# Merging the up-projection tiles and loading their gate tiles as side steps

## The chip, the cores and the metric

The kernel runs on one core of a Trainium2 chip. The metric is the device time of one launch in microseconds (us). The engines named here are TensorE (PE for its matmuls, PEld for its weight loads), VectorE (DVE), ScalarE (ACT), GpSimd (POOL) and SyncE (SP), which issues most of the DMAs.

## The reference

The reference is one decoder block in float32: 512 tokens, model width 2048. The part that matters here stands at its end. Two branches, retention and sparse attention, each give an array of 512 x 1024. Each is widened to 2048 columns, multiplied by its own sigmoid gate, and the two are added:

```
merged = sigmoid(m_a) * (y_ret @ w_up_ret) + sigmoid(m_b) * (y_nsa @ w_up_nsa)
x = x + gate[:, None] * (merged @ w_out)
return rmsnorm(x, g_final)
```

`gate` is a third of a projection of the conditioning vector `c` through `w_ada`.

## The kernel before, in words

**Stages.** The kernel first forms the modulated input, then streams the input projection through TensorE group by group, with the two attention branches worked off beside it; then comes the up stage, which the change touches, and then the output projection. Every large product is done as three products of rounded parts: a weight is split into a high part `whi` (ACT rounds it, L261) and a low part `wlo` (DVE subtracts, L262), and a product is high x high, high x low and low x high (L414).

**The up stage (L1005 to L1020).** It has eight groups, in the order j = 0 to 3 and, for each j, first w = 1 (sparse attention, weights `w_un`) and then w = 0 (retention, weights `w_ur`). A group makes four result tiles `u` of 128 channels x 512 tokens in four PSUM banks. It uses four weight tiles of 128 x 1024 (512 KB), called W1 to W4 below, and each holds two of the eight contraction steps. So a group is 4 tiles x 8 steps x 3 = 96 matmuls. `run_group` (L431) does them in three blocks: W1 alone, W2 alone, then W3 and W4 together (tail=2). A block (L423) runs four steps, one per result tile; after each step it calls `tick`. In the last block each step closes its tile, and the evacuation `ev` of that tile is written out at once.

**Evacuation (L990 to L1003).** For w = 1 it is one DVE product, `mtmp = u * sg` (L993). For w = 0 it is the product `sg = u * sg` (L996), the sum into `mtmp` (L997), ACT's rounding to the high part `mhi` (L1000) and DVE's subtraction to the low part (L1001); for j of 2 and 3 POOL then stores the low part to DRAM (L1003).

**The gates' tiles.** `sg` is a tile of 256 KB with the sigmoid of one gate, which the input projection stored to DRAM in `ma_d`. Each group loads its four `sg` tiles on SP's queue (L1017) before its first block is written out. They share four buffers, so the load of one waits until the evacuation of the tile before it in that buffer has read it.

**The gate column.** Between the weights of the up stage stand 32 more tiles of 512 KB, four in each group, called g1 to g4 below. Each is one DVE step into `gacc` (L987).

**What sets the order.** Each engine works off its queue in the order of the program. `load` (L218, issue at L236) keeps up to five raw 512 KB tiles in flight or in use, in the order W1 g1 W2 g2 W3 g3 W4 g4; a load is written out as soon as a buffer has been taken before it, and on the chip it waits until that use is over. `split` (L251) keeps three pairs of `whi`, `wlo`. Written out, block 1 splits W2 and W3, block 2 splits W4, and block 3 splits W1 of the next group; g1 follows block 1, g2 and g3 follow block 2, g4 follows block 3. SP's loads are written out g3 at block 1, W4 and g4 at g1, the next W1 with block 2, the next g1 and W2 behind it, the next g2 at block 3, the next W3 at g4.

**Side steps.** `side` is a queue of functions. `tick(w)` (L377) adds rate x w to a credit, which is never above 2.0, and runs one side step for each whole credit; `flush` (L383) runs what is left. `tick` is called with w = 1 in blocks 1 and 2 and with w = 2 in block 3. In the kernel before, the queue is empty throughout the up stage; the output projection fills it with four loads of `x` and four short products of the gate column, at a rate of 0.5.

Of the kernel before, what the change touches and what calls it, by code (L numbers as in the profile page):

```python
# [16 lines left out]
OP = mybir.AluOpType  # L17
# [68 lines left out]
def block_kernel(ctx: ExitStack, tc: tile.TileContext, t_in, out):  # L86
    nc = tc.nc
# [14 lines left out]
    def gbank(name):  # L102
        return bank("pg", 4, name)
# [10 lines left out]
    def bigt(name, dt=F32):  # L114
        return big.tile([P, 8, 512], dt, tag="big", name=name)
# [256 lines left out]
    side = deque()  # L372
    credit = [0.0]
    RATE_N, RATE_R = 0.32, 0.2
    rate = [0.0]
# [7 lines left out]
    def flush():  # L383
        while side:
            side.popleft()()
# [45 lines left out]
    def run_group(grp, idx, n, between=None, tail=2):  # L431

        items = []
        done = 0
        while done < n:
            if plan[idx][0] not in "wh":
                between(idx, plan[idx])
                idx += 1
                continue
            items.append(idx)  # L440
            idx += 1
            done += 1
            if done <= n - tail or done == n:
                grp.block(items)
                items = []
        while idx < len(plan) and plan[idx][0] not in "wh":
            between(idx, plan[idx])
            idx += 1
        return idx
# [524 lines left out]
    y_lo["r"] = bigt("ylo_r", F32R)  # L974
    for h in range(RH):
        nc.gpsimd.dma_start(y_lo["r"][:, h, :], yl_d[0, h])
    m_hi = [None, None]
    m_lo = [None, None]

# [10 lines left out]
    def up_evac(w, j, sgs):  # L990
        def ev(t, b):
            if w:
                nc.vector.tensor_tensor(mtmp[:, t, :], b, sgs[t], op=OP.mult)  # L993
                return
            a, k8 = divmod(4 * j + t, 8)
            nc.vector.tensor_tensor(sgs[t], b, sgs[t], op=OP.mult)  # L996
            nc.vector.tensor_tensor(mtmp[:, t, :], sgs[t], mtmp[:, t, :], op=OP.add)  # L997
            hs = m_hi[a][:, k8, :]
            ls = wk.tile([P, 512], F32R, tag="p", bufs=3, name=f"ml{j}{t}") if a else m_lo[0][:, k8, :]
            nc.scalar.copy(hs, mtmp[:, t, :])  # L1000
            nc.vector.tensor_tensor(ls, mtmp[:, t, :], hs.bitcast(F32), op=OP.subtract)  # L1001
            if a:
                nc.gpsimd.dma_start(ml_d[k8], ls)  # L1003
        return ev

    for j in range(4):
        if j % 2 == 0:
            m_hi[j // 2] = bigt(f"mhi{j}", F32R)
            if j == 0:
                m_lo[0] = bigt("mlo0", F32R)  # L1010
        for w in (1, 0):
            bk = [gbank(f"u{j}{w}_{t}") for t in range(4)]
            yh, yl = y_hi["n" if w else "r"], y_lo["n" if w else "r"]
            sgs = []
            for t in range(4):
                sg = wk.tile([P, 512], F32, tag="ev", bufs=4, name=f"sg{j}{w}{t}")
                nc.sync.dma_start(sg, ma_d[w, 4 * j + t])  # L1017
                sgs.append(sg)
            grp = Group("F", bk, lambda kk, y=yh: y[:, kk, :], lambda kk, y=yl: y[:, kk, :], 8, up_evac(w, j, sgs))
            idx = run_group(grp, idx, 4, gate_item)  # L1020


    m_lo[1] = bigt("mlo1", F32R)
# [146 lines left out]
```

## Time and profile before

| | us |
|---|---|
| median of 3 runs (1617.72 to 1619.35) | 1617.76 |
| the profiled execution's own time | 1619.62 |
| its span, first to last instruction | 1617.9 |
| PE busy in it | 1588.0 (98%) |
| DVE busy | 712.6 (44%) |
| ACT busy | 489.2 (30%) |
| the up stage, first to last product, start to start | 1253.10 to 1429.78 |

The profile's page tells busy time per engine and the chain of work that ended last; it is 90% PE. Beside the page, the trace can be asked for the waits between engines, for the instructions of one engine in order of time with the idle time ahead of each, and for the busy time, granted TensorE clock and DMA rate of any stretch. Matmuls are pipelined, so the distance between the starts of two matmuls, not the length of one, tells how fast they follow each other. An SP row gives the time for which SP issued a transfer; the landing is later.

### The profile page before, as it was taken

The numbers are of one execution on the slowest core, as the hardware profiler recorded it, in microseconds if no ns is written. First come the engines' busy times: TensorE is split into PE (matmuls) and PEld (weight loads), VectorE is DVE, ScalarE is ACT, GpSimd is POOL, SyncE is SP. The second block draws the span as 40 slices with busy tenths as digits, with TensorE's granted clock in tenths as the row PEclk, the third lists the DMA queues.
The fourth block names the chain that finished last, engine by engine and source line by source line (L and its number), as shares of the span: only waits on it lengthen the run. The fifth ranks groups of instructions, "written<-read, shape, count | busy, mean of one in ns | idle before, by whom it ended". The sixth has DMA issues, their size and how long they took to land.

```text
span 1617.9 us, 18828 instructions
## 1 busy us (share of the span) xinstructions
PE 1588.0 (98%) x7502; PEld 1266.3 (78%) x7502; DVE 712.6 (44%) x1238; ACT 489.2 (30%) x719; POOL 33.9 (2%) x68
## 2 busy tenths in 40 slices
PE   7999999999999999999999999999999999999997
PEld 2566777888888888778888888888888888778886
DVE  5454533345534344542245343332221566654444
ACT  1223313234433534432333333332222222222223
POOL 2000000000000000000001000000001000010000
PEclk9999999999999999999999999999999999999999
DMA  9886354323323313213544554333335777884322
GB/s 373 325 312 222 112 172 152 105 91 106 103 72 98 105 59 98 92 59 111 172 143 134 178 179 147 122 124 124 112 112 167 271 230 236 260 297 182 104 79 105
DMA packets 88217, 252.54 MB, mean 156 GB/s; under 512 B 9248, under 2 KB 18528, under 8 KB 86976
## 3 DMA queue, kind: packets, MB, share of 16 engines
q1 hardware_dynamic: 80048, 235.71, 42.5%
q0 software_dynamic: 7504, 13.53, 2.7%
q10 hardware_dynamic: 576, 2.10, 0.3%
q8 instruction: 59, 0.97, 0.2%
q14 instruction: 30, 0.25, 0.0%
HBM read 224.03 MB, written 27.26 MB: 155 GB/s over the span
## 4 chain that ended last, share of the span: by engine, by line
PE 90%; DVE 4%; DMA 3%; ACT 2%; issue 1%; SPq 0%; ACTq 0%; DVEq 0%
PE g L414 58%; PE o L414 11%; PE u L414 6%; PE g L879 2%; PE o L719 2%; PE sc L682 2%; PE pa L324 2%; PE tp L705 1%; PE ssq L272 1%; PE phid L603 1%; DMA raw<-in_w_ada 1%; DVE wlo L262 1%; DMA raw<-in_w_un 1%; DMA raw<-in_w_ur 1%; PE o L716 1%
## 5 line engine op out<-in xcount | busy, mean ns | idle before, releaser
L262 DVE TENSOR_TENSOR wlo<-raw,whi 128x1024 fp32r<-128x1024 f32 x246 | 297.9, 1223 | 487.0 <-ACT whi L261 486.9
L414 PE MATMUL g<-hhi,whi 128*128 128x512 f32 x1088 | 438.2, 403 | 0.0
L414 PE MATMUL g<-hhi,wlo 128*128 128x512 f32 x1088 | 424.8, 390 | 1.6 <-DVE wlo L262 1.6
L414 PE MATMUL g<-hlo,whi 128*128 128x512 f32 x1088 | 424.1, 390 | 0.0
L261 ACT CAST whi<-raw 128x1024 fp32r<-128x1024 f32 x246 | 255.0, 1048 | 499.8 <-PE g L414 229.0
L414 PEld LDWEIGHTS g<-hhi,whi 128*128 128x128 f32 x1088 | 204.7, 188 | 56.2 <-issue 11.6
L414 PEld LDWEIGHTS g<-hhi,wlo 128*128 128x128 f32 x1088 | 204.5, 188 | 46.4 <-DVE wlo L262 2.5
L414 PEld LDWEIGHTS g<-hlo,whi 128*128 128x128 f32 x1088 | 204.8, 188 | 42.9 <-issue 1.4
L414 PE MATMUL g<-whi,hhi 128*128 128x512 f32 x320 | 133.8, 418 | 0.0
L414 PE MATMUL g<-wlo,hhi 128*128 128x512 f32 x320 | 124.9, 390 | 1.2 <-DVE wlo L262 1.2
L414 PE MATMUL g<-whi,hlo 128*128 128x512 f32 x320 | 125.0, 391 | 0.0
L414 PE MATMUL o<-whi,mhi 128*128 128x512 f32 x240 | 95.0, 396 | 0.0
L414 PE MATMUL o<-wlo,mhi 128*128 128x512 f32 x240 | 93.5, 390 | 0.0
L414 PE MATMUL o<-whi,mlo 128*128 128x512 f32 x240 | 93.4, 389 | 0.0
L414 PEld LDWEIGHTS g<-wlo,hhi 128*128 128x128 f32 x320 | 60.2, 188 | 16.7 <-issue 2.4
L414 PEld LDWEIGHTS g<-whi,hhi 128*128 128x128 f32 x320 | 60.1, 188 | 15.8 <-issue 3.2
L414 PEld LDWEIGHTS g<-whi,hlo 128*128 128x128 f32 x320 | 60.0, 188 | 13.0
L685 DVE CUSTOM_DVE_ANT_0 p<-sc,c_mask 128x128 f32<-128x128 f32 (+3 forms) x64 | 31.2, 488 | 85.3 <-PE sc L682 85.2
L706 ACT COPY pT<-tp 128x128 f32<-128x128 f32 (+3 forms) x64 | 27.3, 426 | 114.6 <-PE tp L705 114.4
L687 ACT ACTIVATE p<-p,sm 128x128 f32<-128x128 f32 (+3 forms) x64 | 36.1, 563 | 75.6 <-DVE sm L685 75.5
L414 PEld LDWEIGHTS o<-wlo,mhi 128*128 128x128 f32 x240 | 45.0, 188 | 10.6 <-issue 1.0
L719 PEld LDWEIGHTS o<-pT,vt 128*128 128x128 f32 x320 | 44.8, 190 | 10.9 <-issue 5.3
(238 smaller groups left out, 1699.8 us busy)
## 6 DMA issues: line engine op xcount, KB each, us to landing
raw<-in_w_in SPq DMA_DIRECT2D x176, 512.0 KB, 3.7
raw<-in_w_ada SPq DMA_DIRECT2D x32, 512.0 KB, 7.7
raw<-in_w_ada SPq DMA_DIRECT2D x16, 1024.0 KB, 8.1
raw<-in_w_gate SPq DMA_DIRECT2D x32, 512.0 KB, 4.7
raw<-in_w_o SPq DMA_DIRECT2D x32, 512.0 KB, 4.4
raw<-in_w_c SPq DMA_DIRECT2D x16, 512.0 KB, 4.1
raw<-in_w_un SPq DMA_DIRECT2D x16, 512.0 KB, 5.1
sg<-ma_d SPq DMA_DIRECT2D x32, 256.0 KB, 3.5
```

The source lines that it names most:

```text
L261: nc.scalar.copy(hi, r)
L262: nc.vector.tensor_tensor(lo, r, hi.bitcast(F32), op=OP.subtract)
L272: nc.tensor.matmul(ssq, ones, sq, start=kk == 0, stop=kk == NK - 1)
L324: nc.tensor.matmul(pa[j][32 * u:32 * u + 32, :], sc32[:, 4 * b + u, :], rs[u // 2][:, u % 2, :], start=b == 0, stop=b == 3)
L414: nc.tensor.matmul(self.banks[t], l, r, start=kk == 0 and n == 0, stop=kk == self.nk - 1 and n == 2)
L603: nc.tensor.matmul(hid[64 * v:64 * v + 64, :], wins[v, s][:, i, :], craw[v][:, i, :], start=s == 0 and i == 0, stop=s == 7 and i == 3)
L682: nc.tensor.matmul(b[:, :n], qT[:, h, t], res["kT"][:, 2 * br + g, :n], start=True, stop=True)
L685: nc.vector.tensor_tensor_reduce(p[:, :n], b[:, :n], mask[:, 512 - n:], -SCALE, 3.0e38, OP.add, OP.min, sm[:, 0:1])
L687: nc.scalar.activation(p[:, :n], p[:, :n], AF.Exp, bias=sm[:, 0:1], scale=-1.0, accum_out=sm[:, 1:2])
L706: nc.scalar.copy(pT[:, :n], b[:, :n])
L719: nc.tensor.matmul(o[:, r * P:(r + 1) * P], res["v"][:, m, 256 * br + P * g:256 * br + P * g + P], pT[:, m * P:(m + 1) * P], start=k == fi ...
L879: nc.tensor.matmul(b, l, r, start=u == 0 and m == 0, stop=u == 3 and m == 2)
```

## The change

It sets the rate to 0.5 for the up stage, takes the sum, the high part and the low part of a w = 0 tile out of the evacuation and puts them in the queue of side steps as `merge(t)`, and puts the four `sg` loads of a group in the same queue instead of issuing them ahead of the group. A `flush` follows the last group.

```diff
+    rate[0] = 0.5
     m_hi = [None, None]
...
             if w:
                 nc.vector.tensor_tensor(mtmp[:, t, :], b, sgs[t], op=OP.mult)
                 return
+            nc.vector.tensor_tensor(sgs[t], b, sgs[t], op=OP.mult)
+            side.append(lambda: merge(t))
+
+        def merge(t):
             a, k8 = divmod(4 * j + t, 8)
-            nc.vector.tensor_tensor(sgs[t], b, sgs[t], op=OP.mult)
             nc.vector.tensor_tensor(mtmp[:, t, :], sgs[t], mtmp[:, t, :], op=OP.add)
             hs = m_hi[a][:, k8, :]
...
             sgs = []
-            for t in range(4):
+
+            def sg_load(t, w=w, j=j, sgs=sgs):
                 sg = wk.tile([P, 512], F32, tag="ev", bufs=4, name=f"sg{j}{w}{t}")
                 nc.sync.dma_start(sg, ma_d[w, 4 * j + t])
                 sgs.append(sg)
+            side.extend([lambda t=t, f=sg_load: f(t) for t in range(4)])
             grp = Group("F", bk, lambda kk, y=yh: y[:, kk, :], lambda kk, y=yl: y[:, kk, :], 8, up_evac(w, j, sgs))
             idx = run_group(grp, idx, 4, gate_item)
+
+    flush()
```

## Rows read from the trace of the kernel before

**Rows 1.** The page's first two parts: TensorE's busy time and granted clock by slices.
```profile
PE 1588.0 (98%) x7502; PEld 1266.3 (78%) x7502; DVE 712.6 (44%) x1238; ACT 489.2 (30%) x719; POOL 33.9 (2%) x68
...
PEclk9999999999999999999999999999999999999999
```
**Rows 2.** Waits, 1250 to 1440 us: who waited for whom, total, times, longest.
```profile
PEld u L414 <- DVE wlo L262: 2.4, 5, 1.0
...
PEld o L414 <- DVE wlo L262: 0.4, 1, 0.4
```
**Rows 3.** PE in order of time (start, length): first products of six groups.
```profile
1253.10 0.39 PE L414 MATMUL u<-yhi_n,whi 128*128 128x512 f32 x1
...
1296.62 0.39 PE L414 MATMUL u<-yhi_n,whi 128*128 128x512 f32 x1
...
1318.73 0.39 PE L414 MATMUL u<-yhi_r,whi 128*128 128x512 f32 x1
...
1340.49 0.39 PE L414 MATMUL u<-yhi_n,whi 128*128 128x512 f32 x1
...
1408.02 0.39 PE L414 MATMUL u<-yhi_r,whi 128*128 128x512 f32 x1
...
1429.78 0.39 PE L414 MATMUL o<-whi,mhi 128*128 128x512 f32 x1
```
**Rows 4.** SP's queue in order of time, loads of the up stage.
```profile
1254.55 1.84 SPq L1017 DMA_DIRECT2D sg<-ma_d  x4
...
1256.92 0.42 SPq L236 DMA_DIRECT2D raw<-in_w_un  x1
...
1290.54 8.44 SPq L1017 DMA_DIRECT2D sg<-ma_d  x4
1301.23 0.33 SPq L236 DMA_DIRECT2D raw<-in_w_gate  x1
1302.37 0.33 SPq L236 DMA_DIRECT2D raw<-in_w_un  x1
...
1313.73 6.23 SPq L1017 DMA_DIRECT2D sg<-ma_d  x4
1320.84 0.33 SPq L236 DMA_DIRECT2D raw<-in_w_gate  x1
1321.98 0.33 SPq L236 DMA_DIRECT2D raw<-in_w_ur  x1
```
**Rows 5.** SP's own waits, 1245 to 1440 us.
```profile
SPq L236 <- DVE wlo L262: 35.2, 32, 2.4
SPq L236 <- DVE gacc L987: 27.4, 29, 2.2
```
**Rows 6.** ACT in order of time: the copy of W4 in three groups.
```profile
1263.10 1.05 ACT L261 CAST whi<-raw 128x1024 fp32r<-128x1024 f32 x1 [7.32 <-DMA raw<-in_w_un]
...
1307.17 1.05 ACT L261 CAST whi<-raw 128x1024 fp32r<-128x1024 f32 x1 [5.98 <-DMA raw<-in_w_un]
...
1327.28 1.05 ACT L261 CAST whi<-raw 128x1024 fp32r<-128x1024 f32 x1 [7.24 <-DMA raw<-in_w_ur]
```
**Rows 7.** DVE in order of time, 1299 to 1342 us.
```profile
1299.92 1.28 DVE L987 SCALAR_TENSOR_TENSOR gacc<-raw,sc,gacc 128x1024 f32<-128x1024 f32 x1
...
1308.25 1.23 DVE L262 TENSOR_TENSOR wlo<-raw,whi 128x1024 fp32r<-128x1024 f32 x1 [3.58 <-ACT whi L261]
...
1328.36 1.23 DVE L262 TENSOR_TENSOR wlo<-raw,whi 128x1024 fp32r<-128x1024 f32 x1 [4.08 <-ACT whi L261]
...
1333.03 0.69 DVE L996 TENSOR_TENSOR sg<-u,sg 128x512 f32<-128x512 f32 x1
...
1341.15 0.68 DVE L996 TENSOR_TENSOR sg<-u,sg 128x512 f32<-128x512 f32 x1
```
**Rows 8.** Stretches: busy time (x instructions) per engine, PEclk, DMA share, GB/s.
```profile
1276.00:1299.00 23.00, 23.00 (x103) 19.06 (x102) 16.41 (x19) 4.30 (x6) 0.00 (x0) 1.00 0.71 228
...
1300.00:1302.00 2.00, 2.00 (x10) 1.67 (x9) 2.00 (x3) 1.19 (x2) 0.00 (x0) 1.00 0.25 82
```

## The prediction, made before the changed kernel ran

> **What bounds the kernel now.** I read the page first: PE is busy for 1588 of 1617.9 us at the full granted clock [rows 1], so a change away from PE can only save what PE loses in waits, and costs only what new waits it makes. How much the up stage loses is read from the starts of the groups' first products. A group without a wait lasts 1340.49 - 1318.73 = 21.76 us, which over 96 matmuls is 0.2267 us each [rows 3]. Eight of them would take 174.08 us; the stage takes 1429.78 - 1253.10 = 176.68 [rows 3]. So 2.60 us are lost there, and that is all the stage could give back. The waits tell on what: PE's weight loads wait for DVE's low parts, five times, and once more at the start of the output projection [rows 2].
>
> Which low part it is follows from the order of products. W4's low part is first used by the 9th matmul of block 3, after 24 + 24 + 8 = 56 matmuls, 12.70 us into a group. In the w = 1 group that starts at 1296.62 this is 1309.32; DVE finishes W4 at 1308.25 + 1.23 = 1309.48 [rows 7]. It is late, and the group lasts 22.11 us. In the w = 0 group from 1318.73 the need is at 1331.43 and W4 is ready at 1329.59: 1.84 us to spare [rows 3, 7].
>
> The chain to W4 runs back over DMA to DVE. SP issues g3 at 1301.23, when the gate step g4 of the group before has freed its buffer (1299.92 + 1.28 = 1301.20) [rows 4, 5, 7]. I call this moment T. W4 is issued at 1302.37, T + 1.14, when DVE has split W2. ACT begins its copy when the data have landed, at 1307.17 = T + 5.94, and the low part is ready at T + 8.25 [rows 4, 6, 7]. In the w = 0 group T is 1320.84 and ACT begins at 1327.28 = T + 6.44.
>
> The old `sg` loads do not stand in this chain. The four of a group occupy SP from 1290.54 to 1298.98 while it waits for one evacuation after another, and g3 behind them waits until 1301.23 for DVE anyway [rows 4, 5]. They move their data just when the DMA engines have least to do: 0.25 of their time is used in 1300 to 1302, against 0.71 over the group [rows 8].
>
> **The change, part by part.**
>
> *The merge.* I follow the credit. After its four loads, which are gone in block 2 at the latest, a group's side queue is empty and block 2 brings the credit to 1.0 (w = 1) or 1.5 (w = 0). Block 3 adds 1.0 per step up to the limit of 2.0, so a w = 1 group ends on 2.0. In a w = 0 group the first tile's product appends its merge, the tick behind it lifts the credit to 2.0, and the merge runs there and then; it leaves 1.0, the next tick makes it 2.0 again. All sixteen merges run straight behind their products, and the last flush finds nothing. DVE, ACT and POOL get the same order as before: no gain, no cost. The credit left is 1.0 instead of 2.0 when the output projection starts, which moves its short gate products by one step of 6 matmuls: 0 us, since each is needed only by evacuations at the end of that group.
>
> *The loads.* With 2.0 credits a w = 0 group runs loads 0 and 1 after the first step of block 1 and load 2 after the third; a w = 1 group, starting with 1.0, runs them after steps 1, 2 and 4. Load 3 comes in block 2. On SP the order was sg, sg, sg, sg, g3, W4, g4, W1'; it becomes g3, sg, sg, sg, W4, g4, W1', sg. Nothing holds the three back once g3 is issued, as their buffers were read before T, so they are issued right at T, ahead of the transfer that is the latest in the group. SP meanwhile sits idle at the boundary where it used to load them.
>
> What that costs W4 is bounded by these rows. *From below:* only SP's issue, at 1.84 / 4 = 0.46 us each [rows 4]: W4 goes out at about T + 0.46 + 3 x 0.46 = T + 1.84 instead of T + 1.14, 0.70 us later, and in w = 0 groups 0.50 less, because there the old fourth `sg` load, which ended only at 1319.96, made the landing 6.44 - 5.94 us longer. *From above:* three transfers of 262,144 bytes at 228 / 0.71 = 321 GB/s [rows 8], 0.82 us each, all in front: 2.46 and 1.96 us. *Nearest row:* the first group, where four `sg`, g3 and W4 were issued back to back from 1254.55 and ACT got W4 at 1263.10 [rows 4, 6]. That is 8.55 us for this very queue with one `sg` more; less 0.82 it is 7.73. Against 5.94 and 6.44 W4 comes 1.79 us later in a w = 1 group and 1.29 in a w = 0 group. I take these.
>
> The Trainium skill's page "DMA: Bandwidth & Descriptors", section Specifications, gives a core about 358 GB/s from HBM. By that an `sg` tile would take 0.73 us (an estimate), the two delays would be 1.88 and 1.38, and the sum below 11.2 instead of 10.5; no stretch here shows more than the rows give, and I keep the rows.
>
> *Where the delay ends.* In a w = 1 group W4 has no time to spare, so PE stands for all of it. In a w = 0 group 1.84 us are to spare and PE doesn't stand, but DVE is busy without a break from W4's subtraction on: two gate steps, the next W1, then the evacuations. These follow one another every (1341.15 - 1333.03) / 3 = 2.71 us [rows 7], and PE's steps of 12 matmuls take 2.72, so DVE never makes up what it is late; the delay reaches gate step g4 and with it the next T, later against PE. The next w = 1 group pays it on top: first W2's low part, then W4's. If a delay is over 1.84 us, PE pays the excess in the w = 0 group and the rest in the next; the sum is the same. After the last group W2 of the output projection, which already makes PE wait [rows 2], takes the place of the next T.
>
> Evacuation waits for nothing new: load 3, the latest, is issued about 4 us after T and its tile is needed over 20 us into the group. The first w = 1 group costs 0: it had the burst already.
>
> *Sum:* three w = 1 groups x 1.79 + four w = 0 groups x 1.29 = 5.37 + 5.16 = 10.5 us. The losses of before, 2.60 us, stay in it. The profiled span would go from 1617.9 to 1628.4, that execution from 1619.62 to 1630.1, and the median, 1.86 below that execution, from 1617.76 to 1628.3.
>
> **The rivals.**
>
> *Issue only.* The DMA engines take W4 beside the `sg` tiles and only SP's issue counts: 3 x 0.70 + 4 x 0.20 = 2.9 us, 1620.7. For it: in 1300 to 1302 three quarters of the DMA time is free. Against it: the first group's burst.
>
> *All in front.* The three tiles add their full time: 3 x 2.46 + 4 x 1.96 = 15.2 us, 1633.0. For it: the DMA engines are the path from T to W4's landing. Against it: the burst was faster.
>
> *Not slower.* SP's queue at the group's start is the place. W4 overtakes the `sg` tiles, or these, no longer loaded while the group before ends, leave it a free way: it lands as before or earlier. From a landing below T + 5.8 on, the w = 1 groups lose nothing, and the stage's waits go: at most 2.60 us, 1615.2. For it: the longer landing in w = 0 groups shows that the old loads were in the way by 0.50. Against it: there it was one tile, now three are closer. The Trainium skill, same page, section "Queues, rings and completion order", has a rule for either side: each DMA engine takes one issuer's descriptors in ring order (W4 waits), but a later transfer may finish before an earlier one (W4 might not).
>
> **How the numbers follow.** Forecast 0.62, issue only 0.17, all in front 0.10, not slower 0.11. About 0.2%, 3.2 us, is what a measurement can tell from no change. The forecast and all in front are slower by more than that, and so is two thirds of issue only, which is likely to be exceeded a little: 0.62 + 0.10 + 0.11 = 0.83. "Not slower" reaches 3.2 us only if something beyond the stage's waits goes: 0.03 faster. The rest, 0.14, is within. The range goes from just below issue only to just above all in front, 1620.5 to 1634.
>
> **What would show it.** SP's rows: g3, then three `sg` rows and W4 within about 2 us. DVE, ACT and POOL: the same order as before. ACT's copy of W4 about 7.7 us after g3's issue. The w = 1 groups for j of 1 to 3 last some 25 us or more, with PE waiting for low parts in block 2 and block 3; w = 0 groups stay at 21.8. It would be wrong if W4 landed within 6.5 us of g3, if merges ran inside the next group's blocks, or if w = 0 groups grew instead.

## The result and the profile after

| | before | changed |
|---|---|---|
| median of 5 runs, us | 1617.76 (1616.51 to 1619.35) | 1634.03 (1631.01 to 1635.47) |
| ratio, 95% interval | | 1.0096 [1.0081, 1.011] |
| profiled execution, us (span) | 1619.62 (1617.9) | 1634.03 (1632.3) |
| up stage, start to start of products, us | 176.68 | 189.19 |

The change costs 16.3 us, with an interval of about 13 to 18. Of the 14.4 us between the two profiled spans, 12.5 lie in the up stage and 1.6 behind it, where PE's first wait in the output projection takes 1.59 us; 0.3 stood before the stage began.

The waits of the changed kernel, 1250 to 1440 us (total, times, longest), answer to [rows 2]. PE and its weight loads wait longer for low parts and often for high parts. The rows of PEld and of PE are in part the same waits, seen on two engines, and are not to be added up.

```profile
PEld u L414 <- DVE wlo L262: 8.0, 6, 1.8
...
PEld u L414 <- ACT whi L261: 5.5, 4, 2.0
PE u L414 <- DVE wlo L262: 5.4, 6, 1.4
...
PE u L414 <- ACT whi L261: 4.0, 3, 1.6
```

In the kernel before, the same view has one wait for a high part in the stage:

```profile
PEld u L414 <- ACT whi L261: 0.9, 1, 0.9
```

PE in order of time: the first products of six groups, as in [rows 3], the waits of the first bad one, and the first wait of the output projection.

```profile
1253.39 0.39 PE L414 MATMUL u<-yhi_n,whi 128*128 128x512 f32 x1
...
1296.92 0.39 PE L414 MATMUL u<-yhi_n,whi 128*128 128x512 f32 x1
...
1304.39 0.50 PE L414 MATMUL u<-yhi_n,wlo 128*128 128x512 f32 x1 [1.38 <-DVE wlo L262]
...
1312.67 0.50 PE L414 MATMUL u<-yhi_n,whi 128*128 128x512 f32 x1 [1.60 <-ACT whi L261]
...
1313.93 0.53 PE L414 MATMUL u<-yhi_n,wlo 128*128 128x512 f32 x1 [0.53 <-DVE wlo L262]
...
1324.73 0.39 PE L414 MATMUL u<-yhi_r,whi 128*128 128x512 f32 x1
...
1346.49 0.39 PE L414 MATMUL u<-yhi_n,whi 128*128 128x512 f32 x1
...
1420.82 0.39 PE L414 MATMUL u<-yhi_r,whi 128*128 128x512 f32 x1
...
1442.58 0.39 PE L414 MATMUL o<-whi,mhi 128*128 128x512 f32 x1
...
1450.01 0.50 PE L414 MATMUL o<-wlo,mhi 128*128 128x512 f32 x1 [1.59 <-DVE wlo L262]
```

The w = 1 group of j = 1 lasts 1324.73 - 1296.92 = 27.81 us instead of 22.11, with a wait in block 2 (W2's low part) and two in block 3 (W4's parts). The w = 0 group behind it still lasts 21.76. All four w = 0 groups do, and so does the first group; j = 2 takes 25.21 and j = 3 27.37 in their w = 1 groups.

SP's queue in the same two groups, against [rows 4]; g3's issue is T.

```profile
1303.23 0.33 SPq L236 DMA_DIRECT2D raw<-in_w_gate  x1
1303.61 1.37 SPq L1022 DMA_DIRECT2D sg<-ma_d  x3
1305.09 0.36 SPq L236 DMA_DIRECT2D raw<-in_w_un  x1
...
1326.84 0.33 SPq L236 DMA_DIRECT2D raw<-in_w_gate  x1
1327.22 1.38 SPq L1022 DMA_DIRECT2D sg<-ma_d  x3
1328.71 0.36 SPq L236 DMA_DIRECT2D raw<-in_w_ur  x1
```

ACT's copy of W4 there, against [rows 6].

```profile
1311.57 1.04 ACT L261 CAST whi<-raw 128x1024 fp32r<-128x1024 f32 x1 [8.40 <-DMA raw<-in_w_un]
...
1334.74 1.05 ACT L261 CAST whi<-raw 128x1024 fp32r<-128x1024 f32 x1 [8.98 <-DMA raw<-in_w_ur]
```

W4 is issued at T + 1.86 instead of T + 1.14, and the copy begins at T + 8.34 instead of 5.94 in the w = 1 group and at T + 7.90 instead of 6.44 in the w = 0 group. Read in the same way for the seven groups after the first, the landing is later by 2.40, 1.50 and 1.10 in the w = 1 groups of j = 1 to 3, and by 1.71, 1.46, 1.41 and 1.62 in the four w = 0 groups: 5.0 + 6.2 = 11.2 us.

The rest is PE's clock. Stretches behind W4's wait in the w = 1 groups of j = 1, 2 and 3 (busy times as in [rows 8]; the third number from the end is the granted clock):

```profile
1313.90:1317.90 4.00, 3.97 (x10) 3.12 (x11) 4.00 (x4) 1.04 (x1) 0.00 (x0) 0.57 0.68 203
...
1361.00:1371.60 10.60, 9.84 (x42) 7.86 (x43) 6.64 (x7) 2.28 (x3) 0.00 (x0) 1.00 0.71 250
1410.20:1413.30 3.10, 3.04 (x7) 2.46 (x8) 3.10 (x4) 1.04 (x1) 0.00 (x0) 0.51 0.62 192
```

In j = 1 and 3 the clock was granted at 0.57 and 0.51 over these stretches, that is mostly at the lower of its two levels, 1.2 GHz; the products there follow one another every 0.427 us instead of 0.227, as these two starts, six products apart, show.

```profile
1314.26 0.62 PE L414 MATMUL u<-yhi_n,whi 128*128 128x512 f32 x1
...
1316.82 0.63 PE L414 MATMUL u<-yhi_n,whi 128*128 128x512 f32 x1
```

At full clock the same work would have taken 4.00 x 0.43 + 3.10 x 0.49 = 3.2 us less. 11.2 + 3.2 = 14.4 is the difference of the spans; since 0.3 of that difference stood before the stage, the account closes to about 0.3 us.

### The profile page after: what moved, and what is told of

Read it like the earlier page. It is cut to its first block, busy times and chain, and to the rows that moved or that the text cites. A ratio compares the mean times of both kernels' runs of the same rounds, so it can differ in the third digit from the quotient of the medians.

```text
span 1632.3 us, 18829 instructions
## 1 busy us (share of the span) xinstructions
PE 1592.4 (98%) x7502; PEld 1268.1 (78%) x7502; DVE 712.6 (44%) x1238; ACT 489.2 (30%) x719; POOL 34.3 (2%) x68
## 4 chain that ended last, share of the span: by engine, by line
PE 86%; DVE 5%; DMA 4%; ACT 2%; issue 2%; SPq 0%; ACTq 0%; DVEq 0%
PE g L414 57%; PE o L414 10%; PE u L414 4%; PE g L879 2%; PE o L719 2%; PE sc L682 2%; PE pa L324 2%; DMA raw<-in_w_un 2%; DVE wlo L262 1%; PE tp L705 1%; PE ssq L272 1%; DMA raw<-in_w_ada 1%; PE phid L603 1%; DMA raw<-in_w_ur 1%; DVE mtmp L1001 1%
## 5 line engine op out<-in xcount | busy, mean ns | idle before, releaser
L414 PE MATMUL u<-yhi_n,wlo 128*128 128x512 f32 x128 | 51.7, 404 | 5.4 <-DVE wlo L262 5.4
L414 PE MATMUL u<-yhi_n,whi 128*128 128x512 f32 x128 | 51.4, 402 | 4.0 <-ACT whi L261 4.0
```

The source lines that it names most:

```text
L414: nc.tensor.matmul(self.banks[t], l, r, start=kk == 0 and n == 0, stop=kk == self.nk - 1 and n == 2)
```

## The experiments

Each time is compared with the kernel before, run on the same chip.

**The merge alone.** The loads go back ahead of the group; the merge stays a side step.

```diff
-            side.extend([lambda t=t, f=sg_load: f(t) for t in range(4)])
+            for t in range(4):
+                sg_load(t)
```

> The merge as a side step alone; the four loads of the gates' tiles stand ahead of each group again. Theory (the credit lets every merge run straight behind its product, so only the moved loads cost): the order on DVE, ACT and POOL is that of the kernel before and the time is its time, ratio 1.000, within 2 us of 1617.8. Rival (merges as side steps cost something themselves, as a part of the 16.3 us): 4 us or more above the kernel before.

Measured: 1618.01 us, ratio 1.0005 [0.9996, 1.0013]. DVE's, ACT's and POOL's instructions stand in the order of the kernel before. The merge part of the change costs nothing that can be told (the interval ends at 2.1 us); the loss is the loads'.

This run also shows how far the landing of W4 differs between executions of the same order. The first two rows are g3's issue and the copy of W4 in the w = 1 group of j = 3 in the kernel before, the last two the same here.

```profile
1389.23 0.33 SPq L236 DMA_DIRECT2D raw<-in_w_gate  x1
1396.45 1.05 ACT L261 CAST whi<-raw 128x1024 fp32r<-128x1024 f32 x1 [7.27 <-DMA raw<-in_w_un]
...
1388.68 0.33 SPq L236 DMA_DIRECT2D raw<-in_w_gate  x1
1394.39 1.05 ACT L261 CAST whi<-raw 128x1024 fp32r<-128x1024 f32 x1 [5.75 <-DMA raw<-in_w_un]
```

The copy begins at T + 7.22 in the one and at T + 5.71 in the other, and the group lasts 23.51 and 21.95 us. Counted against this profile instead of that of the kernel before, the seven landings of the changed kernel are later by 14.0 us in all, not 11.2.

**The loads of w = 0 alone.**

```diff
-            side.extend([lambda t=t, f=sg_load: f(t) for t in range(4)])
+            if w:
+                for t in range(4):
+                    sg_load(t)
+            else:
+                side.extend([lambda t=t, f=sg_load: f(t) for t in range(4)])
```

> Only the loads of the w = 0 groups are side steps; those of w = 1 stand ahead again. Theory (a late W4 in a w = 0 group makes DVE's evacuations late, and the next group pays): W4's copy starts 7.9 to 8.1 us after g3's issue in the w = 0 groups, which still last 21.8 us; PE stands in the w = 1 groups of j = 1 to 3, in block 2 too, where the loads were not moved, and at the start of the output projection; 4 x 1.55 = 6.2 us, 1624, plus up to 3 if the granted clock falls after the waits. Rival (each group pays for its own late W4, and a w = 0 group has 1.84 us to spare): no loss, 1618.

Measured: 1623.35 us, ratio 1.004 [1.0026, 1.0054]. PE in order of time, waits over 0.6 us:

```profile
1301.87 0.50 PE L414 MATMUL u<-yhi_n,wlo 128*128 128x512 f32 x1 [1.10 <-DVE wlo L262]
...
1346.73 0.51 PE L414 MATMUL u<-yhi_n,wlo 128*128 128x512 f32 x1 [0.70 <-DVE wlo L262]
...
1392.18 0.50 PE L414 MATMUL u<-yhi_n,wlo 128*128 128x512 f32 x1 [1.37 <-DVE wlo L262]
...
1436.88 0.50 PE L414 MATMUL o<-wlo,mhi 128*128 128x512 f32 x1 [1.11 <-DVE wlo L262]
```

All of them read `yhi_n`, or lie in the output projection: PE stands in the w = 1 groups, where nothing was moved, in block 2, and at the start of the output projection. The w = 0 groups last 21.76 to 21.92 us. The rival would have had no loss. So a late W4 in a w = 0 group is paid by the group after it. W4's copy came at T + 7.4 to 8.2, a wider spread than expected.

**The loads of w = 1 alone.** The same edit with the two cases exchanged.

> Only the loads of the w = 1 groups are side steps. Theory: W4 lands about 7.5 to 8.3 us after g3's issue in w = 1 groups, PE waits in block 3 of j = 1 to 3 and not in block 2: 3 x 1.67 = 5.0 us, 1622.8, plus up to 1.7 for each group in which the granted clock falls. Rival (the loss passes through DVE in w = 0 groups alone): 1618.

Measured: 1624.93 us, ratio 1.0053 [1.004, 1.0066]. PE waits in block 3 alone, as here in j = 1, and in j = 2 and 3 alike; no product ran at half pace.

```profile
1309.97 0.50 PE L414 MATMUL u<-yhi_n,whi 128*128 128x512 f32 x1 [1.39 <-ACT whi L261]
...
1311.23 0.50 PE L414 MATMUL u<-yhi_n,wlo 128*128 128x512 f32 x1 [0.53 <-DVE wlo L262]
```

The copy came at T + 8.1 to 8.5, and these groups last 24.25 to 24.41 us, so they lose more than the 1.67 us each that I had taken from the changed kernel; the time is 2.1 us above the expected 1622.8. The two halves add up to 0.93%, against 0.96% for both.

**The loads behind the next W1.** They are side steps still, but enter the queue behind g1, at a rate of 1.0.

```diff
-    rate[0] = 0.5
+    rate[0] = 1.0
+    late = []
...
                                            op0=OP.mult, op1=OP.add)
+        side.extend(late)
+        late.clear()
...
-            side.extend([lambda t=t, f=sg_load: f(t) for t in range(4)])
+            late.extend([lambda t=t, f=sg_load: f(t) for t in range(4)])
```

> The four loads are side steps of block 2, so that SP issues them behind W4, g4 and the next W1. Theory (only their place ahead of W4 costs): W4's copy starts 5.9 us after g3's issue in w = 1 groups as before, in w = 0 groups about 5.9 instead of 6.4; no new waits of PE; 1615.5 to 1618.5. Rival (loads issued inside a group cost wherever they stand, because they share the DMA engines with the weights): 1622 or more.

Measured: 1616.55 us, ratio 0.9994 [0.9986, 1.0003]. In the w = 0 group of j = 1 SP's rows and ACT's copy of W4 are these:

```profile
1319.75 0.33 SPq L236 DMA_DIRECT2D raw<-in_w_gate  x1
1320.89 0.33 SPq L236 DMA_DIRECT2D raw<-in_w_ur  x1
1322.02 0.33 SPq L236 DMA_DIRECT2D raw<-in_w_gate  x1
1323.22 0.33 SPq L236 DMA_DIRECT2D raw<-in_w_un  x1
1323.60 2.04 SPq L1025 DMA_DIRECT2D sg<-ma_d  x4
```

```profile
1325.77 1.05 ACT L261 CAST whi<-raw 128x1024 fp32r<-128x1024 f32 x1 [7.11 <-DMA raw<-in_w_ur]
```

The copy starts at T + 6.02 here, T + 5.82 on average over the w = 0 groups and 5.99 over the w = 1 groups, and every group lasts 21.76 to 21.83 us. The same four transfers inside the group cost nothing once W4 goes first; the rival falls. The same kernel once more:

> The kernel with the four loads behind the next W1 once more, to narrow its interval. Theory (it takes away the waits of the kernel before in the w = 1 groups, some 1 to 2.5 us): 0.9985 to 0.9995 of the kernel before. Rival (no different from it): 0.9998 to 1.0005.

Measured: 1615.91 us, ratio 0.9995 [0.9986, 1.0004]. Its stage lasts 174.39 us, without the losses of [rows 3], but the runs can't tell about 1 us from none. A version that is better than the kernel before is not shown.

**One load ahead, three behind.**

```diff
-            late.extend([lambda t=t, f=sg_load: f(t) for t in range(4)])
+            side.append(lambda f=sg_load: f(0))
+            late.extend([lambda t=t, f=sg_load: f(t) for t in range(1, 4)])
```

> One load of the gates' tiles stays ahead of W4, the other three go behind the next W1. Theory (W4 comes later by the bytes ahead of it): the copy starts about 0.6 to 0.8 us later than with none ahead, at 6.5 to 6.8 us after g3's issue; the w = 0 groups are as late as in the kernel before, so three w = 1 groups pay 0.7 each: 1618 to 1620. Rival (any load in front costs the whole 1.5 to 2.4 us): 1625 or more.

Measured: 1619.92 us, ratio 1.0011 [1.0001, 1.0022]. The copy starts at T + 6.43 on average in w = 0 groups and 6.33 in w = 1 groups, 0.61 and 0.34 later than with none ahead, with W4's issue unmoved at T + 1.14 in all but one group. In w = 1 groups that is less than expected. The copy in the w = 0 group of j = 1:

```profile
1320.77 0.33 SPq L236 DMA_DIRECT2D raw<-in_w_gate  x1
...
1327.28 1.05 ACT L261 CAST whi<-raw 128x1024 fp32r<-128x1024 f32 x1 [7.60 <-DMA raw<-in_w_ur]
```

Three ahead make the copy 2.15 and 2.07 later in the changed kernel (T + 7.97 and 8.06). The delay grows with the number of tiles in front; this run can't tell whether by their number or by their bytes.

**A quarter of the bytes.** The same places in the queue, 64 KB each.

```diff
-                nc.sync.dma_start(sg, ma_d[w, 4 * j + t])
+                nc.sync.dma_start(sg[:, :128], ma_d[w, 4 * j + t, :, :128])
```

> The changed kernel with each gate tile's load cut to a quarter of its columns (64 KB), at the same places in SP's queue; the evacuations use the quarter four times, so the gates are wrong. Theory (W4 waits for the bytes ahead of it): W4's copy starts about 6.6 us after g3's issue in all groups, so 3 x 0.7 + 4 x 0.2 = 2.9 us are left of the loss and no fall of the granted clock: 1618 to 1621. Rival (three more transfers in the queue cost W4 by their number, not by their bytes): copy still about 8 us after g3's issue, 1630 or more.

Measured: 1625.53 us, ratio 1.0043 [1.0029, 1.0056]. In the w = 0 group of j = 1, SP's rows and ACT's copy:

```profile
1322.05 0.33 SPq L236 DMA_DIRECT2D raw<-in_w_gate  x1
1322.43 1.38 SPq L1030 DMA_DIRECT2D sg<-ma_d  x3
1323.92 0.36 SPq L236 DMA_DIRECT2D raw<-in_w_ur  x1
```

```profile
1329.15 1.05 ACT L261 CAST whi<-raw 128x1024 fp32r<-128x1024 f32 x1 [8.18 <-DMA raw<-in_w_ur]
```

The copy still starts at T + 6.9 to 7.8, 7.25 on average in w = 0 groups and 7.61 in w = 1 groups. Both accounts are wrong: with a quarter of the bytes over half of the delay is left.

**A quarter of the rows.** 64 KB again, as 32 rows of 2 KB.

```diff
+    sgp = [ev_tile(f"sgp{t}") for t in range(4)]
+    for a in sgp:
+        nc.gpsimd.memset(a, 0.5)
...
-                sg = wk.tile([P, 512], F32, tag="ev", bufs=4, name=f"sg{j}{w}{t}")
-                nc.sync.dma_start(sg, ma_d[w, 4 * j + t])
-                sgs.append(sg)
+                nc.sync.dma_start(sgp[t][0:32, :], ma_d[w, 4 * j + t, 0:32])
+                sgs.append(sgp[t])
```

> The changed kernel with each gate tile's load cut to 32 of its 128 partitions: 64 KB as in the quarter by columns, but in 32 rows of 2 KB instead of 128 rows of 512 bytes, into four tiles that stay the same through the stage, so the gates are wrong. The quarter by columns left W4's copy 6.9 to 7.8 us after g3's issue. Theory (what was left there is the price of the rows, each partition's row being a packet, beside SP's issue): with a quarter of the rows only SP's issue is left, the copy at about 6.5 us in all groups, 1618 to 1621. Rival (each transfer in front has a price of its own, whatever its rows and bytes): copy at 6.9 to 7.8 us as before, about 1625.

Measured: 1625.19 us, ratio 1.0046 [1.0033, 1.006]; the copy at T + 7.05 on average in w = 0 groups and 7.69 in w = 1 groups. In the w = 1 group of j = 1:

```profile
1300.84 0.33 SPq L236 DMA_DIRECT2D raw<-in_w_gate  x1
...
1308.24 1.05 ACT L261 CAST whi<-raw 128x1024 fp32r<-128x1024 f32 x1 [7.44 <-DMA raw<-in_w_un]
```

My theory of the rows falls: fewer rows change little. Of the 1.2 to 1.7 us by which three of 64 KB delay W4 against none, 0.73 is SP's issue (T + 1.87 instead of T + 1.14); the other 0.5 to 1.0, some 0.2 to 0.3 each, comes between issue and landing. For the three tiles of 256 KB of the changed kernel the same subtraction leaves 1.3 to 1.4, or 0.45 to 0.47 each. So part of the price goes with the bytes and part does not; an estimate of 0.20 us for 64 KB, by the 321 GB/s worked out from [rows 8], lies within what was measured for the small ones, but the same rate gives 0.82 for a tile of 256 KB, which is too much. In which part of the DMA path the price arises was not tried. The Trainium skill's page "DMA: Bandwidth & Descriptors", section Bandwidth, measures 0.95 us of DMA time for 64 KB and 6.15 for 1 MB on GpSimd's path, so that a small transfer costs more than its bytes there too; the traces agree in kind, with 0.2 to 0.3 us for 64 KB beside 0.45 to 0.47 for 256 KB.

**PE's waits filled.** Idle products into a bank that nothing reads, in the w = 1 groups of j = 1 to 3: 6 ahead of W2's first low part, 10 ahead of W4's first product.

```diff
                     for n, (l, r) in enumerate(ops):
+                        if t == 0 and self.fill and (kk, n) in ((2, 2), (6, 0)):
+                            fb = sbank("fill")
+                            l0 = splits[ks[0][1]][0][:, 0:P]
+                            for _ in range(6 if kk == 2 else 10):
+                                nc.tensor.matmul(fb, l0, ah, start=True, stop=True)
...
+            grp.fill = bool(w and j)
```

> The changed kernel with 6 and 10 idle products into an unread bank in the w = 1 groups of j = 1 to 3, where PE waits in block 2 and block 3 (1.4 and 2.3 us of work). Theory (the granted clock falls because PE has stood twice in a short time, and that costs what the sum of the landings does not explain): no product at half pace in these groups, none over 26.3 us, and the time 2 to 4 us below the changed kernel on the same chip, though work was added. Rival (the clock is not the cause, or falls for reasons of its own): the time of the changed kernel or up to 3 us above.

Measured: 1633.48 us, ratio 1.0093 [1.0078, 1.0109], and the changed kernel beside it:

> The changed kernel itself, for comparison on this chip: about 1634, 1.0096 of the kernel before; a wait in block 2 and in block 3 of the w = 1 groups of j = 1 to 3, and products at half pace behind some of these waits.

Measured: 1634.78 us, ratio 1.0096 [1.0081, 1.0111]. The w = 1 group of j = 1 as a stretch, with the waits filled:

```profile
1297.00:1326.00 29.00, 28.59 (x125) 22.91 (x124) 16.60 (x20) 7.15 (x9) 0.00 (x0) 1.00 0.56 193
```

and in the changed kernel's first profile:

```profile
1297.00:1325.00 28.00, 24.49 (x99) 19.00 (x98) 15.03 (x18) 6.58 (x8) 0.00 (x0) 0.94 0.53 188
```

With the waits filled the clock stays granted in full, and this group lasts 26.44 us instead of 27.81 and, in the changed kernel's second profile, 28.21. In that second profile the clock fell in j = 1 alone. The groups of j = 2 and 3 last 25.87 and 25.63 us filled, against 25.21 and 27.37 in the first profile of the changed kernel and 25.82 and 25.62 in the second: filling saves time only where the clock had fallen. So three of the six such groups of the changed kernel lost the clock and none of the three filled ones did. That PE's standing takes the clock down fits all of this; one profile with the waits filled does not show it beyond doubt. That it is worth 2 to 4 us of the time is not shown: the medians differ by 1.3 us inside overlapping intervals. W4 happened to land later in this profile (T + 8.58 in the group of j = 1, and a wait of 0.43 us in a w = 0 group). Counted from the first product of the up stage to the end, the filled kernel's profile takes 377.6 us, the changed kernel's two 378.9 and 378.1.

## Why the prediction was right, and where it was short

It said slower by 10.5 us, to 1628.3; it is 16.3, to 1634.03, at the very end of its range. That it lies there is in part luck: the end of the range was set by a rival with another price for the loads, and left no room for the clock. Point by point:

- *The merge moves nothing.* Right: the credit lets each merge run behind its product, and the merge alone measures 1.0005 [0.9996, 1.0013].
- *Three loads go out at T ahead of W4, and W4 lands late.* Right in order and in issue: T + 1.86 where I had T + 1.84.
- *How late.* The first term that was mis-sized. I took the first group's burst, 8.55 us, less one tile at 0.82 us, 7.73, and measured 8.06 on average in w = 1 groups and 7.97 in w = 0 groups; 11.2 us in the sum instead of 10.5. The subtraction was the mistake: the changed kernel's own first group has such a burst with one tile less and needs 8.35.

```profile
1254.63 0.38 SPq L236 DMA_DIRECT2D raw<-in_w_gate  x1
...
1262.98 1.05 ACT L261 CAST whi<-raw 128x1024 fp32r<-128x1024 f32 x1 [6.90 <-DMA raw<-in_w_un]
```

  Over the kept profiles the burst takes 8.55, 8.83 and 9.09 us with four tiles in front (the kernel before, w = 0 alone, the merge alone) and 8.19 to 8.56 in four profiles with three. The row that I took was the shortest of its kind, and by the averages a tile is worth about 0.47 us, not 0.82. I had priced it by its bytes, and with a quarter of the bytes over half of the delay stays. Two readings beside this were off as well. I took 5.94 us as the landing of all w = 1 groups, though j = 3 had 7.22 in the same trace; with that the same sum would have been 9.2. And the 321 GB/s are not the most that the trace shows: the page has 373 GB/s in its first slice.
- *Who pays.* Right: w = 0 groups unchanged, their delay carried through DVE's evacuations to W2 of the next group, and to W2 of the output projection (1.59 us idle there). The evacuations keep their pace, every (1348.61 - 1340.50) / 3 = 2.70 us as in [rows 7]:

```profile
1340.50 0.68 DVE L996 TENSOR_TENSOR sg<-u,sg 128x512 f32<-128x512 f32 x1
...
1348.61 0.68 DVE L996 TENSOR_TENSOR sg<-u,sg 128x512 f32<-128x512 f32 x1
```

- *The clock.* The term that was missing. From the full granted clock [rows 1] I went on to count a wait at its own length. In two of the three w = 1 groups in which PE waited in block 2 and in block 3, the products behind ran at half pace: 3.2 us in the profiled execution, more than the landings were mis-sized by there.
- *The sum.* 11.2 + 3.2 = 14.4 is the profiled difference, to 0.3 us. The median's 16.3 has 14.4 in its interval. The 1.9 us between belong to the profile of the kernel before: that execution, 1619.62, lies 1.86 above its own median, while the changed kernel's profiled execution is its median. Part of what made it longer is seen, the late W4 of j = 3. So 11.2 for the landings is likely a low count; against the merge alone it is 14.0.
- *The rivals.* Issue only (2.9 us) and not slower fall. *All in front* came closest in time, 1633.0, and its 15.2 us of landings is not far above the 11.2 to 14.0 measured. What goes against it is the price of a tile: 0.34 to 0.61 us with one in front and about 0.47 in the burst, where it has 0.82.

## What to carry to other kernels

Ahead of moving a transfer on an in-order queue, find the transfer behind it that has no time to spare: loads that filled an idle moment of the queue for nothing cost 16 us when they were moved to where the queue is the critical path, and nothing when they were put behind that transfer. Price a transfer in front by its issue and by a measured row of its own size, not by its bytes alone, and take such a row from more than one execution. And allow for more than their length where waits of PE come close together: in three of six groups the clock went with them.

## What the runs showed of the hardware that was not expected

Three transfers of 64 KB ahead of one of 512 KB delayed it by 1.2 to 1.7 us, three of 256 KB by 2.1: a quarter of the bytes kept 60 to 80% of the delay, with 128 rows of 512 bytes as with 32 rows of 2 KB.

The granted clock fell behind waits of 1.54, 1.76 and 0.69 us in one group of the changed kernel and of 1.39, 1.78 and 0.69 in another, not behind 1.39, 0.96 and 0.70 in the third (distances of starts less 0.227, which is 0.16 more than the idle time in the rows). In its second profile it fell behind 1.49, 2.29 and 0.69, not behind 1.53, 1.36 and 0.69 or 1.07, 1.70 and 0.69. It did not fall where block 3's waits of 1.5 to 1.7 and 0.7 stood alone, and it stayed at full level where idle products filled the waits.

Ahead of the up stage, where all these kernels are the same, the granted clock differs between executions too. From 20 to 90 us it was 1.00 with the loads of w = 0 alone, 0.95 in the kernel before and the changed kernel, 0.93 in the changed kernel's second profile and 0.90 with the waits filled, and the up stage began at 1251.12, 1253.10, 1253.39, 1254.93 and 1255.07 us. That is up to 4 us between single executions, more than one fall of the clock in the stage costs.
